# One core's hybrid decoder layer: an opening over two HGRN2 units, and recurrences of two HGRN2 units that step together

## The chip, the core and the metric

The kernel runs on one core of a Trainium2 chip. Of the core's engines, PE (TensorE) multiplies matrices into PSUM, DVE (VectorE) and ACT (ScalarE) do elementwise work, POOL (GpSimd) fills tiles, and SP (SyncE) issues most of the DMA transfers. The metric is the time of one execution on the device, in microseconds (us).

## The reference

One decoder layer over a sequence of 2048 tokens with width 1024, in float32, for a batch of one:

```
c_act = silu(c);  mod = c_act @ w_ada + b_ada        # 1024 -> 6 x 1024: sh1, sc1, g1, sh2, sc2, g2
h = rms_norm(x) * (1 + sc1) + sh1
proj = h @ w_in     # retention q k v g | HGRN2 q f v g | GLA q k v g, low-rank gate
x = x + g1 * (concat(retention, HGRN2, GLA) * head_gain) @ w_out
h = rms_norm(x) * (1 + sc2) + sh2
x = x + g2 * conv_gated_mlp(h)
out = rms_norm(x) * final_gain
```

An HGRN2 head forgets with f = lb + (1 - lb) sigmoid(z), has the key (1 - lb) sigmoid(-z) and the query silu(q). Its recurrence is S_t = diag(f_t) S_(t-1) + k_t v_t and o_t = q_t S_t. The output of each head is normalized and multiplied with silu of its gate.

## The kernel before

The sequence is cut in 4 blocks of 512 tokens. In each block the input projection is done unit by unit, in the order h0, h1, g, h2, h3, r0, r1: four HGRN2 units of two heads, one GLA unit (in two halves), and two retention units. The activations h are held as 8 tiles of 128 channels x 512 tokens, each as a high and a low part (`high`, `low`, tiles `ha`), and weights likewise (tiles whose names begin with h and l), so that a product is three multiplications: high x high, high x low, low x high (`split3`). Low parts of weights are kept in DRAM in block 0 (`keep`) and loaded again in later blocks.

An HGRN2 unit (`unit_h`) multiplies f (`pshfh`) and q (`pshqh`) in the layout channels x tokens, and value and gate (`psvgh`) in the layout tokens x channels. In block 0, value and gate of the first two units go unit by unit with 256 columns (`tf_gemm`); all other pairs go together with 512 columns (`tf512`). `tok_evac` and `tok_evac4` copy them out of PSUM: the value by ACT, the gate by ACT (sigmoid) and DVE (product).

The recurrence (`gated`) is a chain of small steps: the products with a token's own key, the dots (`dth`), seven levels with strides 1, 2, ..., 64 (`lvh`, each needing DVE's products of the level before on q and k, `qbh` and `kh`; its result goes by a masked copy into `ath`), the transposed key (`kTh`), the state's updates (`uh`, `S`), the output (`oh`), its normalization (`post`, with a Newton iteration on DVE) and its transposition (`oTh`). A planner, the class `Clock`, adds up modelled TensorE times of the projections as they are written down and inserts the next step of the chain when it is due. One chain runs at a time; the next waits in a line. PE's order is the order in which this is written; DVE, ACT and SP are ordered by a scheduler with priorities, except in the opening.

The opening (`startup`) is written out by hand for PE, DVE, ACT and SP. The condition is loaded as 128 equal rows (`craw`, 512 KB) and squashed on ACT and DVE (`c_act`). `cond(m)` multiplies it with a weight tile `wada` and sums, on DVE; 16 of the 48 such products lie in the opening. The squares of x are made by ACT and added up by DVE in a chain (`san`); TensorE sums them over the channels (`ssn`), DVE makes the reciprocal root (`rsn`), TensorE spreads it (`bcn`), and ACT copies it (`bc`). Then, for the 8 channel tiles k in turn, come scale, high part, low part, and the products of unit h0 (f, q, value and gate) with that tile. Unit h1's products follow from the general code.

PSUM has 4 banks `acc`, 2 `lev` and 2 `late`. Weights have 3 buffers each for high and low parts.

Of the kernel before, what the change touches and what calls it, by code (L numbers as in the profile page):

```python
# [4 lines left out]

# [13 lines left out]
P = 128  # L19
# [32 lines left out]
LEVEL_GAP = (3.2, 4.8)  # L52
# [50 lines left out]
def trunk(ctx, tc, xT, vecs, cvec, cst, rope, msk, wada, win, walow, wgla, wout, wup, wdown, out):  # L103
# [39 lines left out]
    nc.sync.dma_start(vec[:], vecs)  # L143
# [7 lines left out]
    nc.sync.dma_start(c_all[:], cst)  # L151
# [35 lines left out]
    def ada_load(m, early):  # L187
        if early:
            raw = pa.tile([P, D], F32, tag="a4k", name=f"wada{m}")
        else:  # L190
# [85 lines left out]
    def tf_gemm(name, i):  # L276
        if name in ready:
            return ready.pop(name)
        pss = [acc_ps(f"ps{name}_{j}") for j in range(NCH // 2)]
        for half in range(2):  # L280
            hi, lo = piece(win[i + half], f"{name}_{half}", f"i{i + half}")
            for c in range(NCH):
                o = pss[c // 2][:, (c % 2) * 256:(c % 2) * 256 + 256]
                for kk in range(4):
                    k = half * 4 + kk
                    sl = slice(kk * 256, (kk + 1) * 256)
                    cs = slice(c * P, (c + 1) * P)
                    split3(o, (h[k][:, 0, cs], h[k][:, 1, cs]), (hi[:, sl], lo[:, sl]),
                           k == 0 and c % 2 == 0, k == KD - 1 and c % 2 == 1)
                    if kk % 2:  # L290
                        adv(6 * M256)
        return pss

    def tf512(name, i, step=2):

        pss = [acc_ps(f"ps{name}_{c}") for c in range(NCH)]
        for q4 in range(4):
            half, sub = q4 // 2, q4 % 2
            src = win[i + half:i + half + step + 1:step][:, :, sub * 512:(sub + 1) * 512].rearrange("a p n -> p a n")
            with tc.high_priority(offset=50):  # L300
# [7 lines left out]
                one = [f"i{i + half + step * a}l" for a in range(2)]  # L308
                if key in kept:
                    nc.sync.dma_start(flat.bitcast(F32), kept[key][:])  # L310
                elif one[0] in kept:
                    for a in range(2):
                        nc.sync.dma_start(lo[:, a, :].bitcast(F32), kept[one[a]][:, sub * 512:(sub + 1) * 512])
                else:
                    with tc.high_priority(offset=HOT):
                        V.tensor_tensor(lo[:], raw[:], hi[:], op=ALU.subtract)
                    keep(key, flat)
# [70 lines left out]
    def startup():  # L388


        x, W, pending = [], {}, []
        for k in range(KD):
            x.append(x_tile(f"x0_{k}", k))
            nc.sync.dma_start(x[k], xT[0, :, k, :])
        raws = {}

        def weight(name, i, extra=False):
            raw = pw.tile([P, 1024], F32, tag="wraw", name="r" + name, bufs=NRAW)
            nc.sync.dma_start(raw[:], win[i])
            if extra:  # L400
                t = [pa.tile([P, 1024], F32R, tag="a4k", name=n + name) for n in "hl"]
            else:
                t = [pw.tile([P, 1024], F32R, tag="w" + n, name=n[0] + name) for n in ("hi", "lo")]
            W[name] = [*t, raw, i]

        def cast(name):
            S.copy(W[name][0][:], W[name][2][:])

        def low_part(name):
            hi, lo, raw, i = W[name]  # L410
            V.tensor_tensor(lo[:], raw[:], hi[:], op=ALU.subtract)
# [4 lines left out]
        def load(*ms):  # L416
            for m in ms:
                raws[m] = ada_load(m, True)
        load(8, 0)
        weight("f", 1)  # L420
# [7 lines left out]
        ps = late_ps("ssn1_0")  # L428
        for c in range(NCH):
            T.matmul(ps[:, c:c + 1], acc[:, c * P:(c + 1) * P], ones, start=True, stop=True)  # L430
# [3 lines left out]
        cast("f")  # L434
        bc = bc1[0] = new_bc1(0)
        ps = late_ps("bcn1_0")
        for c in range(NCH):
            T.transpose(ps[:, c * P:(c + 1) * P], r[:, c:c + 1].to_broadcast([P, P]), ident)
        cond(0)
        cond(9)  # L440
        S.copy(bc[:], ps[:])
        cast("q")
        pf, pq = acc_ps("pshfh0_0"), acc_ps("pshqh0_0")
        pv = [acc_ps(f"psvgh0_0_{j}") for j in range(NCH // 2)]

        def put(kind, k, w):

            two = (0, 1) if w == 0 else (0,)
            if kind in "fq":
                sl = slice(k * P, (k + 1) * P)  # L450
                for p in two:
                    T.matmul((pf if kind == "f" else pq)[:], W[kind][w][:, sl], h[k][:, p, :],
                             start=k == 0 and w == 0 and p == 0, stop=k == KD - 1 and w == 1, skip_group_check=True)
            else:
                sl = slice((k % 4) * 256, (k % 4 + 1) * 256)
                for c in range(NCH):
                    for p in two:
                        T.matmul(pv[c // 2][:, (c % 2) * 256:(c % 2) * 256 + 256], h[k][:, p, c * P:(c + 1) * P],
                                 W[f"v{k // 4}"][w][:, sl], start=k == 0 and w == 0 and p == 0 and c % 2 == 0,
                                 stop=k == KD - 1 and w == 1 and c % 2 == 1, skip_group_check=True)  # L460

        def flush():
            for q in list(pending):
                if (q[0] if q[0] in "fq" else f"v{q[1] // 4}") in parts[q[2]]:
# [3 lines left out]
        plan = [((10,), (), (1,), "f"), ((3, 11), (), (2,), "q"), ((4,), (10,), (3,), "v0"),  # L468
                ((12, 5), (11,), (4,), None), ((13, 6), (12,), (5,), "v1"), ((14, 7), (13,), (6,), None),
                ((15,), (14,), (7,), None), ((), (15,), (), None)]  # L470
        parts = {"f", "q"}, set()
        for k, (ld, first, then, wl) in enumerate(plan):
            if k == 0:
                weight("v0", 2)
            if k == 3:
                weight("v1", 3, True)
            load(*ld)
            for m in first:
                cond(m)
            scaled(x[k], bc[:], k)  # L480
            high(x[k], k, "0_")
            if k in (1, 4):
                name = "v0" if k == 1 else "v1"
                cast(name)
                parts[0].add(name)
            for m in then:
                cond(m)
            low(x[k], k)
            if wl:
                low_part(wl)  # L490
                parts[1].add(wl)
            pending += [(kind, k, w) for w in (0, 1) for kind in "fqv"]
            flush()
        assert not pending
        ready["hfh0_0"], ready["hqh0_0"], ready["vgh0_0"] = pf, pq, pv
# [47 lines left out]

    def tok_evac(vsg, pss):
        v, sg = vsg
        for j, ps in enumerate(pss):
            p3 = ps[:].rearrange("p (c n) -> p c n", n=256)
            c2 = slice(2 * j, 2 * j + 2)
            S.copy(v[:, c2, :], p3[:, :, 0:P])
# [1075 lines left out]
```

## Time and profile before

| | |
|---|---|
| median of 3 runs | 2557.72 us (2553.83 to 2558.8) |
| profiled execution | 2554.22 us, of which the span 2552.4 us |
| granted TensorE clock, mean | 0.993 |
| busy: PE / DVE / ACT / POOL | 97% / 78% / 45% / 6% |
| chain that ended last | PE 82%, DVE 8%, DMA 5% |

The span goes from the first to the last instruction of the profiled execution. Rows of the timeline give start, duration, engine, line, operation, the tiles written and read, the shapes, and in brackets the idle time before and what ended it. Rows of groups give the busy time of all, the mean in ns of one, then the idle time of the engine before them and what ended it; "x8" is a count. Rows of waits give engine, line, what was waited for, the sum, the number and the longest. Line numbers are those of the kernel before.

### The profile page before, as it was taken

Reading aid. Unit: us, or ns where it says so; the run is one execution under the profiler, and the core shown is the slowest. Engines: PE = TensorE matmul, PEld = TensorE weight load, DVE = VectorE, ACT = ScalarE, POOL = GpSimd, SP = SyncE. Lnnn points to the kernel's source line nnn. Section 1 sums busy time; section 2 is a strip of 40 time slices with the busy share of each in tenths; the row PEclk is TensorE's granted clock in tenths of the full one; section 3 lists DMA queues with packets and bytes.
Section 4 is the critical chain, followed back from the end, with each engine's and each line's share of the span. In section 5 each row is a group of like instructions: output and inputs, shape, how many; then the busy total and the mean of one; then the engine's idle time right before and its main releaser. Section 6 shows DMA issues by size and latency. Waiting matters only on the chain.

```text
span 2552.4 us, 35707 instructions
## 1 busy us (share of the span) xinstructions
PE 2480.7 (97%) x12418; PEld 2088.8 (82%) x12418; DVE 1986.5 (78%) x3654; ACT 1138.9 (45%) x1946; POOL 164.1 (6%) x287
## 2 busy tenths in 40 slices
PE   5999999999999999999999999999999999999998
PEld 4888887888888888888788888888878888888887
DVE  8987887878588685876798888887678778778666
ACT  3333334434353343434464555555445555455442
POOL 1000000000000000000110000000001001000000
PEclk9999999999999999999999999999999999999999
DMA  8843558864689645887655445487675544547663
GB/s 311 284 156 127 167 171 315 291 221 158 201 285 306 215 166 189 305 296 243 203 169 179 152 145 165 145 271 242 215 227 175 156 145 146 148 142 255 217 193 129
DMA packets 233028, 525.05 MB, mean 206 GB/s; under 512 B 25456, under 2 KB 28560, under 8 KB 232848
## 3 DMA queue, kind: packets, MB, share of 16 engines
q1 hardware_dynamic: 229648, 512.28, 60.9%
q0 software_dynamic: 3200, 10.49, 1.2%
q8 instruction: 98, 1.61, 0.3%
q14 instruction: 82, 0.67, 0.1%
HBM read 397.37 MB, written 125.30 MB: 205 GB/s over the span
## 4 chain that ended last, share of the span: by engine, by line
PE 82%; DVE 8%; DMA 5%; issue 1%; ACT 1%; SPq 0%; DVEq 0%; POOL 0%; ACTq 0%; POOLq 0%
PE X L254 6%; PE X L256 6%; PE X L255 6%; PE lvh L637 3%; PE Z L255 3%; PE Z L256 3%; PE Z L254 3%; PE dX L254 3%; PE dX L255 3%; PE dX L256 3%; PE psqkvgr L254 2%; PE psqkvgr L256 2%; PE psqkvgr L255 2%; PE dY L254 2%; PE dY L256 2%; PE dY L255 2%
## 5 line engine op out<-in xcount | busy, mean ns | idle before, releaser
L254 PE MATMUL X<-B,A 128*128 128x512 f32 x572 | 223.4, 391 | 1.4 <-ACT u L1332 1.4
L256 PE MATMUL X<-B,A 128*128 128x512 f32 x572 | 222.8, 390 | 0.0
L255 PE MATMUL X<-B,A 128*128 128x512 f32 x572 | 222.8, 390 | 0.0
L1038 DVE TENSOR_TENSOR dA<-rd,dA 128x512 fp32r<-128x512 f32 x154 | 106.1, 690 | 87.2 <-ACT dA L1037 86.8
L1037 ACT CAST dA<-rd 128x512 fp32r<-128x512 f32 x154 | 95.8, 622 | 140.6 <-PE dY L256 45.7
L1038 DVE TENSOR_TENSOR A<-s,A 128x512 fp32r<-128x512 f32 x176 | 120.6, 686 | 37.8 <-ACT A L1037 37.5
L1037 ACT CAST A<-s 128x512 fp32r<-128x512 f32 x176 | 108.8, 618 | 66.1 <-PE Z L256 43.5
L254 PE MATMUL dX<-dB,dA 128*128 128x512 f32 x352 | 136.9, 389 | 0.0
L255 PE MATMUL dX<-dB,dA 128*128 128x512 f32 x352 | 136.9, 389 | 0.0
L256 PE MATMUL dX<-dB,dA 128*128 128x512 f32 x352 | 136.9, 389 | 0.0
L254 PEld LDWEIGHTS X<-B,A 128*128 128x128 f32 x572 | 107.7, 188 | 24.4 <-ACT u L1332 2.2
L256 PEld LDWEIGHTS X<-B,A 128*128 128x128 f32 x572 | 107.5, 188 | 22.4
L255 PEld LDWEIGHTS X<-B,A 128*128 128x128 f32 x572 | 107.6, 188 | 22.2
L637 PEld LDWEIGHTS lvh<-qbh,kh 128*128 128x128 f32 x896 | 116.3, 191 | 10.7 <-issue 3.5
L255 PE MATMUL Z<-B,A 128*128 128x512 f32 x308 | 120.1, 390 | 2.7 <-DVE B L1038 2.7
L637 PE MATMUL lvh<-qbh,kh 128*128 128x128 f32 x896 | 120.5, 277 | 2.1 <-DVE kh L647 2.0
L254 PE MATMUL Z<-B,A 128*128 128x512 f32 x308 | 119.9, 389 | 0.0
L256 PE MATMUL Z<-B,A 128*128 128x512 f32 x308 | 119.8, 389 | 0.0
L1038 DVE TENSOR_TENSOR dB<-rb,dB 128x512 fp32r<-128x512 f32 x154 | 105.6, 687 | 9.8 <-ACT dB L1037 9.8
L254 PE MATMUL psqkvgr<-hqkvgr,ha 128*128 128x512 f32 x256 | 106.6, 416 | 4.6 <-DVE orsg L160 4.6
L1038 DVE TENSOR_TENSOR A<-r,A 128x512 fp32r<-128x512 f32 x130 | 89.4, 688 | 26.7 <-ACT A L1037 26.7
L1037 ACT CAST A<-r 128x512 fp32r<-128x512 f32 x130 | 81.0, 623 | 61.6 <-PE Z L256 59.4
(461 smaller groups left out, 7021.0 us busy)
## 6 DMA issues: line engine op xcount, KB each, us to landing
gs<-yv SPq DMA_DIRECT2D x154, 256.0 KB, 3.0
rb<-gs SPq DMA_DIRECT2D x154, 256.0 KB, 4.1
r<-wup SPq DMA_DIRECT2D x140, 256.0 KB, 3.5
s<-sumsu SPq DMA_DIRECT2D x136, 256.0 KB, 3.2
wada<-wada SPq DMA_DIRECT2D x48, 512.0 KB, 5.6
rd<-sumsd SPq DMA_DIRECT2D x88, 256.0 KB, 3.9
rd<-wdown SPq DMA_DIRECT2D x66, 256.0 KB, 3.9
x<-xT SPq DMA_DIRECT2D x64, 256.0 KB, 5.7
```

Of the source, the lines that this page charges most:

```text
L254: T.matmul(ps, lhs[0], rhs[0], start=first, stop=False, skip_group_check=more)
L255: T.matmul(ps, lhs[0], rhs[1], start=False, stop=False, skip_group_check=more)
L256: T.matmul(ps, lhs[1], rhs[0], start=False, stop=last, skip_group_check=more)
L637: T.matmul(ps[:, c * P:(c + 1) * P].rearrange("p (h n s) -> p h n s", h=2, s=s), kq[:, c * P:(c + 1) * P], rhs, start=True, stop=True)
L1037: S.copy(hi, src)
L1038: V.tensor_tensor(lo, src, hi, op=ALU.subtract)
```

## The change

**The prelude.** The condition comes as a tile of 128 x 8 (`ccol`, one DMA of single elements), is squashed on that tile, and spread by 8 transposes on TensorE and two copies by ACT. The vectors (`vec`) and constants (`c_all`) are loaded from POOL's queue instead of SP's. x comes by 4 DMAs of two tiles each. DVE adds only two squares each, and TensorE sums the four results into one bank (16 small products instead of 4). The first two scalings read the spread root from PSUM and don't wait for its copy.

**The opening.** It does f and q of h0 and h1, and their value and gate together with 512 columns, in an order written out: `scale(k)` (scale and high part), `rest(k)` (low part, then every product whose parts are there), `get(name)` and `lows(name)` (high and low part of a weight). `tf_gemm` and `tok_evac` are gone.

PE's order at the opening's first chunks before (`hf`, `lf`, `hq`, `lq`: parts of h0's weights for f and q; `hv`, `lv`: its value and gate):

```order
L452 MATMUL pshfh_0_429<-ha_0_440,hf 128x512 x2
L452 MATMUL pshqh_0_430<-ha_0_440,hq 128x512 x2
L452 MATMUL pshfh_0_429<-ha_0_440,lf 128x512
L458 MATMUL psvgh_0_0_431<-hv_435,ha_0_440 128x256 x4
L458 MATMUL psvgh_0_1_432<-hv_435,ha_0_440 128x256 x4
L452 MATMUL pshqh_0_430<-ha_0_440,lq 128x512
L452 MATMUL pshfh_0_429<-ha_1_455,hf 128x512 x2
L452 MATMUL pshqh_0_430<-ha_1_455,hq 128x512 x2
L458 MATMUL psvgh_0_0_431<-hv_435,ha_1_455 128x256 x4
L458 MATMUL psvgh_0_1_432<-hv_435,ha_1_455 128x256 x4
L452 MATMUL pshfh_0_429<-ha_1_455,lf 128x512
L452 MATMUL pshqh_0_430<-ha_1_455,lq 128x512
```

PE's order at the same place now (`pshfh_0` and `hf_372` are h0's, `pshfh_1` and `hf_457` h1's):

```order
L456 MATMUL pshfh_0_447<-ha_0_452,hf_372 128x512 x2
L456 MATMUL pshqh_0_448<-ha_0_452,hq_378 128x512 x2
L456 MATMUL pshfh_0_447<-ha_0_452,lf_373 128x512
L456 MATMUL pshqh_0_448<-ha_0_452,lq_379 128x512
L456 MATMUL pshfh_0_447<-ha_1_473,hf_372 128x512 x2
L456 MATMUL pshqh_0_448<-ha_1_473,hq_378 128x512 x2
L456 MATMUL pshfh_0_447<-ha_1_473,lf_373 128x512
L456 MATMUL pshqh_0_448<-ha_1_473,lq_379 128x512
L456 MATMUL pshfh_1_449<-ha_0_452,hf_457 128x512 x2
L456 MATMUL pshfh_1_449<-ha_1_473,hf_457 128x512 x2
L456 MATMUL pshfh_0_447<-ha_2_495,hf_372 128x512 x2
L456 MATMUL pshqh_0_448<-ha_2_495,hq_378 128x512 x2
```

Value and gate come in only after the fourth chunk; in their place stands f of h1, and behind it q of h1.

**The recurrences.** `gated` takes a list of units. h0 and h1 give one chain, h2 and h3 another, each starting after the odd unit's f and q: at every level the products of both units stand one behind the other. `LEVEL_GAP` is 4.8 for all, instead of 3.2 for a single unit.

ACT's order behind the opening now, from the copy of GLA's low-rank gate `alg` on (`hvgg`: high parts of GLA's value and gate weights; `kg`: GLA's key; `vh_1`, `sgh_1`: value and gate of h1):

```order
L832 COPY alg_877<-alg_860 32x512
L291 CAST hvgg_0_1046<-rvgg_0_1044 128x1024
L291 CAST hvgg_1_1097<-rvgg_1_1095 128x1024
L834 ACTIVATE kg_857<-psakg_889 128x512
L607 COPY vh_1_831<-psvgh_1_0_566 128x128
L608 ACTIVATE sgh_1_832<-psvgh_1_0_566 128x128
L607 COPY vh_1_831<-psvgh_1_1_567 128x128
L608 ACTIVATE sgh_1_832<-psvgh_1_1_567 128x128
L607 COPY vh_1_831<-psvgh_1_2_568 128x128
L608 ACTIVATE sgh_1_832<-psvgh_1_2_568 128x128
L607 COPY vh_1_831<-psvgh_1_3_569 128x128
L608 ACTIVATE sgh_1_832<-psvgh_1_3_569 128x128
```

The copies of h1 out of PSUM stand behind the second `hvgg` cast and `kg`; before, they stood ahead of both.

PE's order at the same place now, from the end of GLA's key (`psakg`) on:

```order
L258 MATMUL psakg_889<-ha_6_667,lakg_880 128x512
L256 MATMUL psakg_889<-ha_7_711,hakg_879 128x512
L257 MATMUL psakg_889<-ha_7_711,hakg_879 128x512
L258 MATMUL psakg_889<-ha_7_711,lakg_880 128x512
L675 MATMUL dth_0_916<-c_all,qkh_0_789 128x2 x4
L675 MATMUL dth_1_925<-c_all,qkh_1_817 128x2 x4
L687 MATMUL lvh_0_1_932<-qbh_0_791,kh_0_777 128x128 x4
L687 MATMUL lvh_1_1_937<-qbh_1_819,kh_1_805 128x128 x4
L256 MATMUL psaqg_960<-ha_0_452,haqg_949 128x512
L257 MATMUL psaqg_960<-ha_0_452,haqg_949 128x512
```

The dots and level 1 of both units stand directly behind `psakg`; before, unit h0's stood among the products of h1.

PE's order at the start of block 1 before (`or`: output of retention; `oTr`: its transposition; `pshfh_1`: f of h1):

```order
L256 MATMUL pshfh_1_3177<-ha_4_2690,lhfh_1_3172 128x512
L579 MATMUL oTr_0_3226<-c_all,or_0_3062 128x128 x4
L626 MATMUL dth_0_3236<-c_all,qkh_0_3152 128x2 x4
L637 MATMUL lvh_0_1_3243<-qbh_0_3154,kh_0_2991 128x128 x4
L254 MATMUL pshfh_1_3177<-ha_5_2696,hhfh_1_3171 128x512
L255 MATMUL pshfh_1_3177<-ha_5_2696,hhfh_1_3171 128x512
L256 MATMUL pshfh_1_3177<-ha_5_2696,lhfh_1_3172 128x512
L254 MATMUL pshfh_1_3177<-ha_6_2702,hhfh_1_3171 128x512
L255 MATMUL pshfh_1_3177<-ha_6_2702,hhfh_1_3171 128x512
L256 MATMUL pshfh_1_3177<-ha_6_2702,lhfh_1_3172 128x512
L254 MATMUL pshfh_1_3177<-ha_7_2708,hhfh_1_3171 128x512
```

PE's order at the same place now (`pshqh_1`: q of h1):

```order
L258 MATMUL pshqh_1_3131<-ha_6_2580,lhqh_1_3126 128x512
L628 MATMUL oTr_0_3203<-c_all,or_0_3050 128x128 x4
L256 MATMUL pshqh_1_3131<-ha_7_2586,hhqh_1_3125 128x512
L257 MATMUL pshqh_1_3131<-ha_7_2586,hhqh_1_3125 128x512
L258 MATMUL pshqh_1_3131<-ha_7_2586,lhqh_1_3126 128x512
L675 MATMUL dth_0_3235<-c_all,qkh_0_3000 128x2 x4
L675 MATMUL dth_1_3244<-c_all,qkh_1_3217 128x2 x4
L687 MATMUL lvh_0_1_3251<-qbh_0_3002,kh_0_2808 128x128 x4
L687 MATMUL lvh_1_1_3256<-qbh_1_3219,kh_1_3016 128x128 x4
L628 MATMUL oTr_1_3267<-c_all,or_1_3179 128x128 x4
L687 MATMUL lvh_0_2_3275<-qbh_0_3002,kh_0_2808 128x128 x4
L687 MATMUL lvh_1_2_3280<-qbh_1_3219,kh_1_3016 128x128 x4
```

The dots and the first two levels of h0 and h1 follow each other behind h1's last q products, where one unit's first level had products of h1 behind it.

The diff, cut to its core:

```diff
-LEVEL_GAP = (3.2, 4.8)
+LEVEL_GAP = 4.8
...
-    nc.sync.dma_start(vec[:], vecs)
+    ccol = pc.tile([P, KD], F32, tag="ccol", name="ccol")
+    with nc.allow_non_contiguous_dma("one row of the condition as columns"):
+        nc.sync.dma_start(ccol[:], cvec.rearrange("o (k p) -> p (o k)", p=P))
+    nc.gpsimd.dma_start(vec[:], vecs)
...
-    nc.sync.dma_start(c_all[:], cst)
+    nc.gpsimd.dma_start(c_all[:], cst)
...
-    craw = pa.tile([P, D], F32, tag="a4k", name="craw")
-    nc.sync.dma_start(craw[:], cvec.to_broadcast([P, D]))
-    S.activation(c_act[:], craw[:], AF.Sigmoid)
-    V.tensor_tensor(c_act[:], c_act[:], craw[:], op=ALU.mult)
...
+        sg = small("csg")
+        S.activation(sg[:], ccol[:], AF.Sigmoid)
+        V.tensor_tensor(ccol[:], ccol[:], sg[:], op=ALU.mult)
+        for j in range(2):
+            ps = lev_ps(f"cb{j}")
+            for n in range(4):
+                T.transpose(ps[:, n * P:(n + 1) * P], ccol[:, 4 * j + n:4 * j + n + 1].to_broadcast([P, P]), ident)
+            S.copy(c_act[:, j * 512:(j + 1) * 512], ps[:])
+        load(8)
+        load(0)
+        weight("f0")
         load(9)
-        weight("q", 0)
-        load(1, 2)
-        acc = new_acc("n1_0")
-        for k in range(KD):
-            sumsq(acc, x[k], k, "n1_0_")
+        weight("q0")
+        load(1, 1)
+        ps = late_ps("ssn1_0")
+        for j in range(4):
+            sq = [tmp(f"sq0_{j}_{n}") for n in range(2)]
+            for n in range(2):
+                S.activation(sq[n][:], x[2 * j + n], AF.Square)
+            V.tensor_tensor(sq[0][:], sq[0][:], sq[1][:], op=ALU.add)
+            for c in range(NCH):
+                T.matmul(ps[:, c:c + 1], sq[0][:, c * P:(c + 1) * P], ones, start=j == 0 and c == 0,
+                         stop=j == 3 and c == NCH - 1, skip_group_check=True)
...
+        def scale(k):
+            scaled(x[k], bps[:] if k < 2 else bc[:], k)
             high(x[k], k, "0_")
+
+        def rest(k):
             low(x[k], k)
+            pending.extend((kind, k, w) for w in (0, 1) for kind in ("f0", "q0", "f1", "q1", "v"))
             flush()
+
+        def lows(name):
+            low_part(name)
+            flush()
+
+        def get(name):
+            cast(name)
+            flush()
+
+        scale(0)
+        lows("f0")
+        weight("f1")
+        get("q0")
+        rest(0)
+        cond(9)
+        load(11)
+        cond(1)
+        load(3, 1)
+        scale(1)
+        lows("q0")
+        weight("q1")
+        rest(1)
+        cond(10)
+        load(12)
+        cond(2)
+        load(4)
+        scale(2)
+        get("f1")
...
+        get("v3")
+        lows("v3")
+        rest(7)
...
         for li, s in enumerate(LEVELS):
+            for one in parts:
+                one.pss = []
+                for q, rows, v, sg in one.subs:
+                    ps = lev_ps(f"lv{one.name}_{s}")
+                    for c in range(NCH):
+                        rhs = q[:, :, c * P:(c + 1) * P].rearrange("p h (n t s) -> p h n t s", t=2, s=s)[:, :, :, 1, :]
+                        T.matmul(ps[:, c * P:(c + 1) * P].rearrange("p (h n s) -> p h n s", h=2, s=s),
+                                 one.kq[:, c * P:(c + 1) * P], rhs, start=True, stop=True)
+                    one.pss.append(ps)
...
             with tc.high_priority(offset=CHAIN):
+                for one in parts:
+                    ev = one.tree[li]
+                    for q, rows, v, sg in one.subs:
+                        qv = q[:].rearrange("p h (n t s) -> p h n t s", t=2, s=s)[:, :, :, 1, :]
+                        V.tensor_tensor(qv, qv, ev[:, :, 0:1].unsqueeze(1).to_broadcast([P, 2, nn, s]), op=ALU.mult)
+                    kv = one.kq[:].rearrange("p (n t s) -> p n t s", t=2, s=s)[:, :, 0, :]
+                    V.tensor_tensor(kv, kv, ev[:, :, 1:2].to_broadcast([P, nn, s]), op=ALU.mult)
...
+            adv(4 * n * MF)
+            yield LEVEL_GAP
...
-        clock.chain(gated(nm, b, u, pos, kq, decay, subs, qk, selh), 9.0 if b == u == 0 else 6.0)
-        if b == 0 and u < 2:
-            tok_evac(subs[0][2:], tf_gemm("vg" + nm, 4 * u + 2))
-            tokens.add(nm)
-            return
+        half.append(SimpleNamespace(name=nm, ui=u, pos=pos, kq=kq, tree=decay[0], cur=decay[1], subs=subs, qk=qk,
+                                    sel=selh))
+        if u % 2:
+            clock.chain(gated(nm, b, [half.pop(0), half.pop(0)]), 9.0 if b == 0 and u == 1 else 6.0)
```

More of the change, by code (lines that the diff above doesn't have):

```diff
@@ new lines, in startup @@
+        weight("v1")
+        rest(3)
+        cond(12)
+        load(14)
+        cond(4)
+        load(6)
+        scale(4)
+        get("v0")
+        lows("v0")
+        weight("v2")
+        rest(4)
+        cond(13)
+        load(15)
+        cond(5)
+        load(7, 1)
+        scale(5)
+        get("v1")
+        cond(14)
+        rest(5)
+        lows("v1")
+        weight("v3")
+        cond(6)
+        scale(6)
+        get("v2")
+        cond(15)
+        rest(6)
+        lows("v2")
@@ L649, in gated @@
+                for ps, at in ((ps, at) for one in parts for ps, at in zip(one.pss, one.attns)):
                     dst = at[:].rearrange("p (a n t s) -> p a n t s", a=8, t=2, s=s)[:, :, :, 1, :]
```

285 lines of the change are left out of this document (122 added, 163 removed).

## The prediction

> **What bounds the kernel now.** I read the page first (the engines and the 40 slices).
>
> ```profile
> span 2552.4 us, 35707 instructions
> PE 2480.7 (97%) x12418; PEld 2088.8 (82%) x12418; DVE 1986.5 (78%) x3654; ACT 1138.9 (45%) x1946; POOL 164.1 (6%) x287
> PE   5999999999999999999999999999999999999998
> ```
>
> TensorE bounds it: it is busy for 97%, and of 40 slices only the first, 64 us long, stands at 5. So a change can win in two ways: less TensorE work, or less of the time in which TensorE waits or runs slowly. The table by stretches says where that time is (start and end, length, then busy time and count of PE, PEld, DVE, ACT, POOL, the granted clock, the DMA share and GB/s); after it I went to the groups by line, the timeline and TensorE's waits.
>
> ```profile
> 0.00:22.28 22.28, 2.98 (x12) 2.50 (x13) 14.77 (x34) 12.22 (x17) 8.29 (x19) 1.00 0.86 310
> 22.28:29.38 7.10, 2.87 (x5) 1.41 (x5) 6.06 (x10) 1.91 (x3) 0.00 (x0) 1.00 0.52 189
> 29.38:58.41 29.03, 25.12 (x140) 21.24 (x140) 26.32 (x38) 8.43 (x12) 1.92 (x2) 1.00 0.89 335
> 58.41:86.05 27.64, 27.23 (x184) 25.16 (x185) 26.82 (x52) 8.17 (x15) 0.00 (x0) 1.00 0.87 305
> 58.41:1240.00 1181.59, 1162.59 (x6523) 998.86 (x6524) 922.18 (x2146) 459.42 (x891) 59.80 (x101) 0.99 0.67 226
> 344.00:352.00 8.00, 6.43 (x39) 5.42 (x38) 8.00 (x20) 2.01 (x3) 0.00 (x0) 1.00 0.36 131
> ```
>
> No weight is multiplied before 22.28 us; five multiplications fit into the next 7.1 us. From 29.38 to 58.41 VectorE is busy for 26.32 of 29.03 us: there TensorE is fed at VectorE's pace. From 58.41 to 1240 us, the other attention work, TensorE idles for only 1181.59 - 1162.59 = 19.0 us: that is all that better stepping can win there, but for the slow clock behind a stall.
>
> **Part 1: up to the first multiplication.** The rows of VectorE around it:
>
> ```profile
> L358 DVE TENSOR_TENSOR san<-san,sqn 128x512 f32<-128x512 f32 x7 | 4.8, 692 | 0.8
> L357 ACT ACTIVATE sqn<-x 128x512 f32<-128x512 f32 x7 | 4.4, 630 | 0.8 <-DVE san L358 0.7
> 19.52 1.28 DVE L199 CUSTOM_DVE_ANT_0 wada<-wada,c_act,vec 128x1024 f32<-128x1024 f32 x1
> 20.72 0.75 DVE L364 SCALAR_TENSOR_TENSOR x<-x,mod,bc 128x512 f32<-128x512 f32 x1
> ```
>
> Three of seven additions go (2.1 us of VectorE), but ScalarE now does a small sigmoid, two copies out of the transposes and eight squares, 8 x 0.63 = 5.0 us, one behind the other; the squares end at about the time at which the additions ended. I take no gain there. Behind the reciprocal root one conditioning product (1.28, the row at 19.52) no longer stands ahead of the first scaling. I take 1.1 us: first multiplication at 21.2 instead of 22.28. Bounds: 2.1 us won if the additions set the pace, 1.5 lost if the constants, which now come over POOL's queue, arrive late at the transposes.
>
> **Part 2: the opening's products.** Spacings of TensorE, full and slow, are read from the timeline:
>
> ```profile
> 59.20 0.39 PE L254 MATMUL pshfh<-ha,hhfh 128*128 128x512 f32 x1
> 63.96 0.39 PE L254 MATMUL pshqh<-ha,hhqh 128*128 128x512 f32 x1
> 68.04 0.95 PE L626 MATMUL dth<-c_all,qkh 128*128 128x2 f32 x8
> 85.69 0.28 PE L254 MATMUL psvgh<-hvgh,ha 128*128 128x256 f32 x1
> 85.81 0.28 PE L255 MATMUL psvgh<-lvgh,ha 128*128 128x256 f32 x1
> 86.05 0.39 PE L773 MATMUL alg<-ha,alow 128*32 128x512 f32 x1
> 169.61 0.68 PE L579 MATMUL oTh<-c_all,oh 128*128 128x128 f32 x4 [3.02 <-DVE oh L573]
> ...
> 170.52 0.63 PE L255 MATMUL pshqh<-ha,hhqh 128*128 128x512 f32 x1
> 170.95 0.63 PE L256 MATMUL pshqh<-ha,lhqh 128*128 128x512 f32 x1
> ...
> 173.74 0.40 PE L254 MATMUL pshqh<-ha,hhqh 128*128 128x512 f32 x1
> 173.97 0.39 PE L255 MATMUL pshqh<-ha,hhqh 128*128 128x512 f32 x1
> ```
>
> 21 multiplications of 512 columns lie between 59.20 and 63.96: 0.227 us each. One of 256 columns takes 0.12 (85.69, 85.81). Before, both HGRN2 units' products are done when `alg` starts at 86.05; in between stand pieces of unit 0's recurrence (dots 0.95, 32 level multiplications and their wait), about 4.6 us that move to later. So the point to compare with is 81.4. After, the same products are 2 x 48 of f and q and 96 of value and gate, all of 512 columns: 192 x 0.227 = 43.6 us (before, with 256 columns, 2 x (48 x 0.227 + 96 x 0.12) = 44.8).
>
> Slow time: behind the wait of 3.02 us at 169.61 the spacing is 0.43 (170.52 to 170.95) until about 173.5; then 0.23 again. So a stall of some 3 us costs about 1.7 us more behind it. VectorE's list decides how many there are after:
>
> ```profile
> L199 DVE CUSTOM_DVE_ANT_0 wada<-wada,c_act,vec 128x1024 f32<-128x1024 f32 x14 | 17.9, 1279 | 1.2 <-DMA wada<-wada 1.2
> L364 DVE SCALAR_TENSOR_TENSOR x<-x,mod,bc 128x512 f32<-128x512 f32 x8 | 6.0, 750 | 0.2
> L371 DVE SCALAR_TENSOR_TENSOR ha<-x,mod,ha 128x512 fp32r<-128x512 f32 x8 | 6.0, 747 | 0.0
> L411 DVE TENSOR_TENSOR lf<-rf,hf 128x1024 fp32r<-128x1024 f32 x1 | 1.2, 1219 | 0.0
> ```
>
> After: 14 conditioning products, 8 scalings, 8 low halves of h and 8 of weights, 17.9 + 6.0 + 6.0 + 8 x 1.22 = 39.7 us of busy time, from 20.1 on: with overlap and some 4 us of waits for casts it ends near 62. The chunks k = 0 to 2 hold 9 x 3 + 3 multiplications, less than VectorE needs for them: I work out two gaps of some 2.5 us (before q0's low half, and at f1's high half, whose cast stands behind that of h[2] on ScalarE), slow clock until about 36, and 1 us at the first value weight. 21.2 + 43.6 + 6.0 of gaps + half of the 9.8 us that run slow, 4.9, is 75.7: 76 against 81.4, **-5.4**. Bounds: with full clock throughout TensorE waits for VectorE's end at 62 plus the last 24 products (5.5), 68: -13. If the slow clock holds until 50, +7 on top: +1.6.
>
> By the Trainium skill (TensorE: Matmul & The Clock Gate, Part 1), the array falls to half rate after an idle window of about 3.4 us and needs about 3.4 us of work for the full rate. The trace agrees in the second (170.0 to 173.5). By the first, gaps of 2.5 us alone need not cool it, and the sum of this part would be nearer -9; I keep -5.4, since the array starts cold.
>
> **Part 3: dots of the first pair.** Behind the opening TensorE does 16 `alg`, 24 `psakg`, then the dots `dth0_0`. These need a PSUM bank that held value/gate of the pair; the copies out of unit 1's half stand on ScalarE behind the cast `hvgg0_1`, which overwrites the weight buffer that `psakg` reads last, and VectorE's `lvgg0_1` stands in the same way before unit 0's last gate products.
>
> ```profile
> L305 ACT CAST hvgg<-rvgg 128x1024 fp32r<-128x1024 f32 x3 | 3.2, 1051 | 2.9 <-PE psaqg L255 2.9
> L316 DVE TENSOR_TENSOR lvgg<-rvgg,hvgg 128x1024 fp32r<-128x1024 f32 x4 | 4.9, 1223 | 0.0
> L558 ACT COPY vh<-psvgh 128x128 f32<-128x128 f32 x8 | 2.1, 266 | 1.0 <-DVE sgh L560 0.7 <-PE psvgh L256 0.3
> L559 ACT ACTIVATE sgh<-psvgh 128x128 f32<-128x128 f32 x8 | 2.3, 288 | 0.0
> ```
>
> So the dots come at psakg's end + 1.05 + 1.15 + three pairs of 0.55 + VectorE's products of 0.4 to 0.7, about 4.5 us, in which TensorE has nothing else in its order; with the slow clock behind it (1.9), **+6.4**. Bounds: 0 if the copies get done before that cast, +8.
>
> **Part 4: start of block 1.** Before, only unit 0's level 1 stands there, with 24 products of unit 1 behind it; TensorE waits 1.57 at the second level pair. After, both units' dots and levels 1 and 2 follow unit 1's last q products with nothing but `oTr` between.
>
> ```profile
> 349.93 1.13 PE L637 MATMUL lvh<-qbh,kh 128*128 128x128 f32 x8 [1.57 <-DVE kh L647]
> L659 DVE COPY_PREDICATED ath<-m_all,lvh 128x512 f32<-128x512 uint32 x80 | 75.8, 947 | 0.0
> L645 DVE TENSOR_TENSOR qbh<-qbh,eh 128x512 f32<-128x512 f32 x96 | 66.0, 688 | 27.2 <-PE lvh L637 26.7
> L647 DVE TENSOR_TENSOR kh<-kh,eh 128x256 f32<-128x256 f32 x96 | 40.2, 418 | 0.0
> ```
>
> A level of a pair costs VectorE 2 x (0.69 + 0.42 + 0.95) = 4.1 us. From `or0_1` on VectorE owes retention's normalization (about 4.7), unit 1's gating (sqh, qkh, two qbh halves: 2.7), a weight's low half (1.2) and the first level, some 12 us, against some 4.5 us of TensorE work in the order: a wait of 6 to 8, of which before had 1.6, plus slow clock: **+5.5**. Bounds +1 (VectorE had done the gating earlier) and +9.
>
> **Part 5: the rest.** Two units in step leave VectorE fewer holes; TensorE's spacing of levels goes from two chains of 7 levels to one. Before's stalls there, of which the largest follow, may go or come again elsewhere:
>
> ```profile
> PE oTh L579 <- DVE oh L573: 3.0, 1, 3.0
> PE psvgh L254 <- DVE sqh L732: 2.6, 1, 2.6
> PE psqkvgr L254 <- DVE orsg L160: 4.6, 2, 2.7
> ```
>
> I take half of these 10.2 us, **-5**; bounds -15 (all 19.0 us but 4) and +4 (blocks 2 and 3 get new ones like part 4's). The loads on POOL's queue, the one DMA instead of two for kept low halves, and 16 instead of 4 one-column products cost nothing: DMA stands at shares under 0.9, and the one-column products lie under ScalarE's squares. From the channel mixer on nothing changes.
>
> **Sum.** -5.4 + 6.4 + 5.5 - 5 = +1.5 on the profiled execution's 2554.22, that is 2555.7; the median of the runs is 3.5 above that profile, so 2559 against it. I say 2558.
>
> **Rivals.**
> - *Faster: the opening keeps up and the stalls of parts 3 and 4 are half as long.* For it: VectorE would end at 62 and TensorE could be done at 68. Against: the order has nothing to fill the two waits. -9 + 3 + 3 - 6 = -9: 2549.
> - *Slower: VectorE at the start of block 1.* If the 12 us of VectorE's list there come in full after `or0_1`, and the same repeats once more where a pair starts (parts 3 and 4 at +8 and +9 with the slow clock, the rest at -3, the opening at -5), the sum is +9: 2567. It decides from a wait of 7 us on at that place. For it: VectorE is busy for all of 8.00 us there before (the row from 344). Against: levels may be taken ahead of other work.
> - *The change does little of what it says*: the order behind the first pair stays the same as before, the waits too; -5 alone, 2552 to 2558.
>
> By a rule on another page of the Trainium skill (DMA: Bandwidth & Descriptors, the at-a-glance table), a load issued by GpSimd has its first byte after about 1 us against 0.6 for SyncE, and pieces under 512 bytes fall behind line rate; the 1024 single elements of the condition and the constants would come later by that, and part 1 would be -0.5. No run here shows it.
>
> **How the numbers follow.** The forecast (terms cancel, 2551 to 2565) gets 0.42: 0.28 of it within 0.2%, 0.04 faster, 0.10 slower. The faster rival gets 0.31, the slower 0.24, the last 0.03 (0.02 of it same, 0.01 faster). That makes faster 0.36, same 0.30, slower 0.34; 0.2%, 5 us, is about what the runs tell from no change, since the three shown span 5.0 us. The range goes from 2545, below the faster rival, to 2568, just above the slower one.
>
> **What would show it.** Right: first multiplication near 21, `alg` near 76, spacing 0.43 until about 36; a wait of about 4.5 us of `dth` for `sgh`'s product behind `psakg`; waits of 6 to 8 us in sum between `or0_1` and block 1's second level. The forecast is wrong if `alg` starts under 70 or over 80, if TensorE's idle time from there to the channel mixer is under 12 us or over 35, or if VectorE's queue, not ScalarE's, is what the dots wait for.

## The result and the profile after

The changed kernel took 2652.43 us (median of 4 runs, 2650.65 to 2654.35), the kernel before 2555.99 beside it. The ratio is 1.0377, with a 95% interval of 1.0359 to 1.0395: 96 us slower, where 2558 was forecast with 2568 as the upper end. From the page of the kernel after:

```profile
span 2652.3 us, 35615 instructions
PE 2529.5 (95%) x12354; PEld 2128.4 (80%) x12354; DVE 1999.9 (75%) x3655; ACT 1139.3 (43%) x1956; POOL 164.6 (6%) x289
PE   6988989999899999999899999999999999999998
PEclk9998979999899999999999999999999999999999
```

TensorE issues 64 instructions fewer and is busy 49 us longer; the granted clock now has an 8 and a 7 in the first six slices, where before it was 9 throughout. To find the place, both executions are cut at the starts of `alg`, GLA's low-rank gate of each block, and at the first product of the up-projection (X). After:

```profile
25.02:80.02 55.00, 49.02 (x192) 38.49 (x193) 42.09 (x62) 15.26 (x20) 7.88 (x12) 1.00 0.92 321
80.02:450.62 370.60, 338.10 (x1787) 290.21 (x1786) 293.29 (x641) 127.37 (x254) 13.88 (x24) 0.92 0.49 167
450.62:776.08 325.46, 306.00 (x1668) 262.46 (x1667) 231.56 (x543) 121.00 (x233) 15.67 (x26) 0.97 0.63 212
776.08:1097.08 321.00, 308.11 (x1671) 264.14 (x1670) 231.51 (x545) 121.13 (x234) 15.67 (x26) 0.97 0.66 224
1097.08:1330.21 233.13, 221.20 (x1227) 189.71 (x1226) 173.83 (x409) 84.51 (x172) 12.07 (x23) 0.97 0.70 240
```

The same cuts of before:

```profile
86.05:402.16 316.11, 306.77 (x1684) 260.71 (x1682) 257.95 (x575) 117.63 (x225) 15.80 (x26) 0.98 0.54 182
402.16:706.32 304.16, 299.94 (x1670) 258.07 (x1671) 228.53 (x544) 122.64 (x238) 15.80 (x26) 0.99 0.69 232
706.32:1007.00 300.68, 297.99 (x1671) 256.16 (x1670) 228.55 (x545) 120.74 (x234) 15.80 (x26) 1.00 0.71 239
1007.00:1233.00 226.00, 223.66 (x1287) 192.96 (x1286) 175.73 (x416) 87.35 (x178) 12.27 (x22) 0.99 0.74 254
```

The opening is 6.0 us shorter (86.05 to 80.02). Block 0 from there on is 54.5 longer (316.1 to 370.6), the next two cuts 21.3 and 20.3, the last 7.1; with 2.7 in the channel mixer that is the 99.9 us between the spans. Part of this is work that lies elsewhere now: in the first cut TensorE has some 100 more of the small products for dots and levels (h0's of block 0, which lay ahead of it before, and h1's of block 1, which lay behind it), in the last 60 fewer. By the prediction's 4.6 us for 40 of them that is an estimated 12 us more and 7 us less. In the first cut TensorE idles for 32.5 us (before 9.3) and its granted clock is 0.92 (before 0.98). From the list of TensorE's waits over the whole execution after (9.1, 5.0, 4.5 and 3.7 lie in the first cut, 7.7 lies in block 1):

```profile
PE oTh L628 <- DVE S L930: 11.2, 4, 4.0
PE psqkvgr L256 <- DVE sgr L609: 9.1, 1, 9.1
...
PE or L642 <- DVE oTh L632: 7.7, 1, 7.7
...
PE psvgh L256 <- DVE sqh L788: 5.0, 1, 5.0
PE dth L675 <- DVE sgh L609: 4.5, 1, 4.5
...
PE dth L675 <- DVE nw L163: 3.7, 1, 3.7
...
```

These end at VectorE, as most of the list does. One was forecast to the tenth (4.5, the first dots), and most others were not forecast at all. From `alg` to the channel mixer TensorE idles for 76.8 us (before 18.6), and the four cuts are 103 us longer in sum; most of the rest is the slower clock behind the waits.

### The profile page after: what moved, and what is told of

The parts are those of the page before. It is cut to its first block, busy times and chain, and to the rows that moved or that the text cites. A ratio compares the mean times of both kernels' runs of the same rounds, so it can differ in the third digit from the quotient of the medians.

```text
span 2652.3 us, 35615 instructions
## 1 busy us (share of the span) xinstructions
PE 2529.5 (95%) x12354; PEld 2128.4 (80%) x12354; DVE 1999.9 (75%) x3655; ACT 1139.3 (43%) x1956; POOL 164.6 (6%) x289
```

## The experiments

Where the kernels' profiled executions stand at the cuts (starts of `alg` in blocks 0 to 3, then X), and the median of their runs:

| kernel | alg 0 | alg 1 | alg 2 | alg 3 | X | us |
|---|---|---|---|---|---|---|
| before | 86 | 402 | 706 | 1007 | 1233 | 2556 |
| after | 80 | 451 | 776 | 1097 | 1330 | 2652 |
| e1 pairs, old opening | 85 | 412 | 732 | 1055 | 1286 | 2609 |
| e2 new opening, one pair | 80 | 442 | 748 | 1053 | 1279 | 2605 |
| e5 old opening, late start | 84 | 440 | 746 | 1052 | 1274 | 2597 |
| e6 after, short Newton | 80 | 443 | 763 | 1081 | 1306 | 2628 |
| e10 new opening, caught up | 80 | 408 | 712 | 1015 | 1240 | 2566 |
| e12 e1, copies first | 85 | 416 | 735 | 1053 | 1286 | 2606 |

**Which half of the change.** Pairs alone (e1):

```diff
 # kernel before, opening unchanged
-        clock.chain(gated(nm, b, u, pos, kq, decay, subs, qk, selh), 9.0 if b == u == 0 else 6.0)
+        half.append(SimpleNamespace(...))
+        if u % 2:
+            clock.chain(gated(nm, b, [half.pop(0), half.pop(0)]), 9.0 if b == 0 and u == 1 else 6.0)
```

> The opening of before, with the recurrences of h0 and h1, and of h2 and h3, stepping together as in the changed kernel. Theory P (the pairing costs the time: two units' state updates, normalizations and transpositions come at once, at the end of a block where VectorE has no holes): 2635 to 2660 us, nearly all of the loss of 96. Rival O (the new opening costs it, by what it delays behind itself): 2550 to 2565.

Measured: 2608.69, ratio 1.0203 (1.0186 to 1.0219).

The new opening, with one pair (e2):

```diff
 # kernel after
-        if u % 2:
+        if not (b == 0 and u < 2):
+            clock.chain(gated(nm, b, [half.pop(0)]), 6.0)
+        elif u % 2:
             clock.chain(gated(nm, b, [half.pop(0), half.pop(0)]), 9.0 if b == 0 and u == 1 else 6.0)
...
-            yield LEVEL_GAP
+            yield LEVEL_GAP if n > 1 else 3.2
```

> The new opening, h0 and h1 as a pair in block 0 alone, every other HGRN2 unit in a chain of its own with the old gap of 3.2. Theory P: the blocks 1 to 3 and the end of block 0 come back to before, 2560 to 2585 (what is left is the stall behind the opening and block 0's pair). Rival O: 2640 to 2655.

Measured: 2605.18, ratio 1.0192 (1.0164 to 1.0220). Both theories were half right: each half costs about 50 us, and 53 + 50 is about the 96 of the whole. In the table e2 stands 40 us behind the kernel before at block 1's `alg` (442 against 402) and loses 6 more up to X (306 and 305 us a block, before 304 and 301). Its profiled execution, at 2612 the longest of four, loses another 12 behind X, where retention's last transposition now comes after X's first product. e1 loses 10 up to block 1's `alg` and then 15, 22 and 5 in the three cuts behind it; of the 10 most are again dots and levels that stand ahead of this `alg` now (some 70 more products in the first cut, 60 fewer in the last).

The condition in e2, `b == 0 and u < 2`, made `u < 2` (e3): pairs of h0 and h1 in all blocks.

> The changed kernel with h0 and h1 as a pair in all four blocks, h2 and h3 in chains of their own. If the end of a block is the place (pair of h2 and h3 running into retention): 2585 to 2610. If the start of a block is (both units' dots and levels behind h1's q): 2630 to 2645. If the two cost alike: about 2615.

Measured: 2599.47, ratio 1.0165 (1.0146 to 1.0184). It is no slower than e2, so the pair at a block's start is not what costs. The pair of h2 and h3 is: with it, in the kernel after, the time is 53 us longer. The old opening with pairs of h0 and h1 in blocks 1 to 3 alone (`b and u < 2`, e8) fits that:

> The opening and block 0 of before; in blocks 1 to 3 h0 and h1 as a pair, h2 and h3 in chains of their own. By the difference of the two kernels with the new opening (2599 with these pairs, 2605 without): 2546 to 2556. If a pair costs at the start of a block what it costs at the end: 2580 to 2600.

Measured: 2559.38 against 2553.32, ratio 1.0022 (1.0013 to 1.0031), 3 us above the expected range: a loss of 6 us, and no gain. In the traces block 1's `alg` comes 8 us later with this pair (450 in e3 against 442 in e2, 411 in e8 against 402 before), since h1's levels stand ahead of it then; by X most of that is made up (1275 against 1279, 1237 against 1233).

**The first dots.** In the changed kernel (e4):

```diff
-                tok_evac4(waiting.pop(one), pss, 256 * i)
+                with tc.high_priority(offset=HOT if b == 0 and u == 1 else 0):
+                    tok_evac4(waiting.pop(one), pss, 256 * i)
```

> The changed kernel, with the copies of h0's and h1's value and gate out of PSUM put ahead of the hvgg cast in block 0. If the wait of 4.5 us of the dots is what part 3 of the prediction says: it goes, with the slow clock behind it, and the time falls by 5 to 7 us, 2645 to 2648. If another wait takes its place: 2652 within 3.

Measured: 2642.58, 10 us less than the kernel after (9 when each is compared with the kernel before beside it), and no wait of the first dots is left. That is some 3 us more than the 6.4 of the wait and its slow clock, a first sign that an early loss grows.

**The line of recurrences.** One number in the kernel before (e5):

```diff
-9.0 if b == u == 0 else 6.0
+22.0 if b == u == 0 else 6.0
```

> The kernel before, with one number changed: the first recurrence (h0 in block 0) starts 13 us later by the planner's clock. Theory L (the recurrences stand in one line that is about as long as a block's projections, so what its start loses comes back as waits at the end of block 0): 2563 to 2571, lost before block 1's low-rank gate starts. Rival (the line has slack): 2553 to 2558.

Measured: 2596.96, ratio 1.0163 (1.0145 to 1.0181): 43.6 us for a start that came 14.5 us later on TensorE. Theory L was right in kind and a factor of three short in size. The chain's position shows how it grows: retention's first step `qTr` in block 0 stands at the end of that line. In before and in e5, the first rows of the timeline for it:

```profile
304.33 0.61 PE L849 MATMUL qTr<-c_all,ra0r 128*128 128x128 f32 x4
```

```profile
82.54 0.95 PE L626 MATMUL dth<-c_all,qkh 128*128 128x2 f32 x8
345.16 0.61 PE L849 MATMUL qTr<-c_all,ra0r 128*128 128x128 f32 x4
```

Started at 82.5 instead of 68.0, it arrives 40.8 late. (The profiled execution of e5, 2604.73 us, is the longest of its four.) The delay grows from unit to unit, as the starts of each one's dots show:

| | h0 | h1 | g | h2 | h3 | `qTr` |
|---|---|---|---|---|---|---|
| before | 68.0 | 109.1 | 149.1 | 225.2 | 264.6 | 304.3 |
| e5 | 82.5 | 123.1 | 169.4 | 250.5 | 298.4 | 345.2 |
| later by | 14.5 | 14.0 | 20.3 | 25.2 | 33.8 | 40.8 |

TensorE's largest waits of e5 between the first two cuts; the second and the third stand in the kernel after too (9.1 and 1.9 there):

```profile
PE ssn L337 <- DVE eh L610: 6.9, 1, 6.9
PE psqkvgr L254 <- DVE sgr L560: 5.8, 1, 5.8
PE pshfh L254 <- DVE sgg L560: 4.2, 1, 4.2
PE oTr L579 <- DVE or L573: 3.9, 1, 3.9
```

Two of them are projections (`psqkvgr`, `pshfh`) that wait until value and gate leave PSUM. ScalarE's rows before the wait of 9.1 in the kernel after and before that of 5.8 in e5 say what those copies wait for in turn:

```profile
254.49 0.79 ACT L608 ACTIVATE sgr<-psqkvgr 128x128 f32<-128x128 f32 x4 [6.82 <-DVE og L622]
257.53 0.79 ACT L559 ACTIVATE sgr<-psqkvgr 128x128 f32<-128x128 f32 x4 [5.10 <-DVE og L573]
```

`og` at L622 (L573 in e5) is the last reader of GLA's gate. The gates have 4 buffers; h2, h3 and GLA's two halves hold them until their recurrences are done. So a late line stops the projections, and these hold up its next steps on TensorE. No run has more of these buffers, so their share in the 41 us stays open.

The start alone does not decide; what counts is where the line stands later on. In e1 it starts 11.6 us later than before (79.7); but as two units step in one chain there, GLA's dots come at 151.4 (before 149.1) and `qTr` at 302.4, not late at all. In the kernel after GLA's dots come at 174.1 and `qTr` at 344.6, much as in e5.

Then the line in the new opening was made to catch up (e9): e2 and e4 together, with smaller gaps between the first pair's levels.

```diff
-            yield LEVEL_GAP if n > 1 else 3.2
+            yield (2.4 if b == 0 and parts[0].ui == 0 else LEVEL_GAP) if n > 1 else 3.2
```

> The new opening with one pair (h0 and h1 in block 0), chains of one unit elsewhere, as in the kernel that took 2605; in addition the copies of value and gate ahead of the hvgg cast, and the planner's gap between the levels of that first pair 2.4 instead of 4.8, so that the line of recurrences is some 20 us earlier from the end of that pair on. Theory L (what the opening costs is the late start of the line): 2555 to 2575, with the waits at the end of block 0 mostly gone. Rival (the opening's order costs by itself, or VectorE can't step faster): 2588 to 2600.

Measured: 2574.71, ratio 1.0074 (1.0058 to 1.0089), 30 less than e2. With 9.0 changed to 3.0 for the pair's start (e10):

> The same, with the first pair due 6 us earlier by the planner (3.0 instead of 9.0 after h1's products). Theory L: another 3 to 10 us if the line was still late, nothing if it had caught up; 2550 to 2570. Rival: a new wait of the dots for the copies out of PSUM takes it back, within 2 of the run before.

Measured: 2565.80, ratio 1.0045 (1.0030 to 1.0059), another 9 less. From its timeline and its waits in block 0:

```profile
306.46 0.61 PE L908 MATMUL qTr<-c_all,ra0r 128*128 128x128 f32 x4
```

```profile
PE dth L675 <- DVE qkh L790: 7.6, 2, 5.2
PE psqkvgr L256 <- DVE orsg L164: 3.0, 1, 3.0
PE ssn L319 <- DVE san L340: 2.2, 1, 2.2
```

`qTr` is back within 2.1 us of before, and of the 50 us 10 are left. So some 40 of the opening's 50 us were the line's. The 7.6 us for which the pair's dots wait belong to the new order itself. No run starts the line of the kernel before earlier, so whether that one would gain from it too is open.

**The pair at a block's end.** From retention's first `qTr` in block 2 backwards and forwards, as a table by stretches: 20 us ahead of it, then up to the transposition of retention's first output, `oTr`. Before:

```profile
885.00:905.10 20.10, 20.10 (x117) 17.42 (x116) 15.17 (x37) 9.92 (x26) 0.13 (x1) 1.00 0.64 206
905.10:933.60 28.50, 28.50 (x172) 25.22 (x172) 27.44 (x71) 13.37 (x20) 5.78 (x10) 1.00 0.46 154
```

e1, pairs with the old opening:

```profile
901.00:921.00 20.00, 20.00 (x125) 17.71 (x124) 9.21 (x33) 5.35 (x13) 1.19 (x3) 1.00 0.42 134
921.00:962.00 41.00, 33.42 (x176) 28.74 (x174) 35.50 (x89) 16.90 (x31) 3.90 (x8) 0.89 0.39 132
```

VectorE's updates of the pair's states in the first stretch of e1:

```profile
L695 DVE SCALAR_TENSOR_TENSOR S<-S,eh,uh 64x64 f32<-64x64 f32 x16 | 4.5, 281 | 9.6 <-PE uh L685 9.2
```

Ahead of `qTr` VectorE has 9.2 us of work instead of 15.2: the pair's state updates wait for TensorE's, one unit after the other, and the first output is there only 5 us before the stretch ends. Behind it VectorE has 35.5 instead of 27.4. By its lines, some 5 of these 8 us are retention's rotations (`ra`, `rb`), which before were done ahead of `qTr`, some 2 the next block's scalings, and 1 the heads' second output. Before, TensorE is busy for all of the 28.5 us of the stretch; in e1 it lasts 41.0, and TensorE idles for 7.6 of them. Less work for VectorE there, first in the kernel after (e6) and then in before (e7):

```diff
-        for _ in range(3):
+        for _ in range(rounds):        # 1 in the heads' normalization, 3 elsewhere
```

> The changed kernel with one round instead of three in the Newton iteration of the heads' normalization (which leaves out two of three rounds, 6 small VectorE instructions of about 0.2 us in each of 8 normalizations of a block). Theory V (where the two units' normalizations come at the end of a block, VectorE's queue sets the end): 15 to 35 us faster, 2617 to 2637, most of it at the ends of the blocks. Rival (TensorE's order or PSUM banks set it): 0 to 6 faster.

> The same edit on the kernel before, as the control. Theory V: the same instructions are covered there, 0 to 6 us faster, 2549 to 2556. If they are as dear there as in the changed kernel, the edit says nothing about pairing.

Measured: 2627.50, 25 less than after; the control 2554.37, ratio 1.0006 (0.9991 to 1.0022). The same instructions are worth 25 us in the kernel after and nothing in the kernel before. But by the table some 8 of the 25 came in block 0, and blocks 1 and 2 stay 320 and 318 long against 304 and 301: shorter iterations mend a quarter or less of what the pairs cost there, and 8 more at the end of block 3.

The rival to a mere excess of work was the order in the queues of VectorE and ScalarE: in block 1 of the kernel after, retention's output `or` waits 7.7 us for `oTh`, whose copies out of both late banks stand among the next block's scalings and behind most of them. e1 has the same wait; e1 with one edit (e12):

```diff
-        S.activation(oT[:, 0, :], ps[:], AF.Copy, scale=hg)
-        V.scalar_tensor_tensor(oT[:, 1, :], ps[:], hg, oT[:, 0, :], op0=ALU.mult, op1=ALU.subtract)
+        with tc.high_priority(offset=CHAIN):
+            S.activation(oT[:, 0, :], ps[:], AF.Copy, scale=hg)
+            V.scalar_tensor_tensor(oT[:, 1, :], ps[:], hg, oT[:, 0, :], op0=ALU.mult, op1=ALU.subtract)
```

> The kernel with the old opening and pairs everywhere (2609), with one edit: the two instructions that take a transposed output out of PSUM (oTh, oTr) come ahead of the next block's scaling in ScalarE's and VectorE's queues. Theory B (at a block's end both late banks hold outputs of the pair, whose copies stand on VectorE behind the next block's scalings, so retention's output on TensorE waits): the wait of 7.7 us in block 1 and its slow clock go, in the other blocks the shorter ones, 2575 to 2592. Rival V (VectorE has too much to do there in sum, whatever its order): 2604 to 2612.

> The same edit on the kernel before, as the control. Theory B: with one unit's output at a time one late bank stays free, so the copy's place is worth little: 2548 to 2558. If the edit helps every kernel alike: 2535 or less.

Measured: 2605.79, ratio 1.0211 (1.0196 to 1.0227), as without the edit; the control (e13) 2555.72, ratio 1.0011 (1.0000 to 1.0022). The waits of `or` are gone, and others stand in their place. TensorE's waits at the end of block 2 in e1, then in e12:

```profile
PE or L594 <- DVE orsr L161: 3.1, 1, 3.1
PE oTh L580 <- DVE S L886: 2.7, 1, 2.7
```

```profile
PE oTr L580 <- DVE orsr L156: 4.3, 1, 4.3
PE oTh L580 <- DVE S L887: 2.7, 1, 2.7
```

In block 1, the place that the theory named, the 7.7 us are gone, `oTr` waits 3.8 and `oTh` 3.4 instead of 2.7, and the block takes 318.8 us instead of 319.2. So theory B fell: the wait went and the time stayed, since the copies come first and the normalization later. That fits the sum of VectorE's work in that stretch as the cause, but doesn't show it: VectorE is idle for 5.5 of the 41.0 us in e1, and for 1.1 of the 28.5 before. How much of the 50 us comes from the steps one behind the other (state update, output, square, normalization) no run separated.

**The sums of squares.** In the changed kernel (e11), the four tiles added up on VectorE and four products instead of sixteen:

```diff
+            if j:
+                V.tensor_tensor(sq[0][:], sq[0][:], last[:], op=ALU.add)
+            last = sq[0]
-            for c in range(NCH):
-                T.matmul(ps[:, c:c + 1], sq[0][:, c * P:(c + 1) * P], ones, ...)
+        for c in range(NCH):
+            T.matmul(ps[:, c:c + 1], last[:, c * P:(c + 1) * P], ones, start=True, stop=True)
```

> The changed kernel with the four tiles of squares added up by VectorE again and four one-column products (eight instructions) instead of sixteen. If those products cost about 0.22 us for each of their 32 instructions on the path, as the profile after shows: VectorE's mean square statistics (msn) start 1.0 to 2.2 us earlier, and the first product of a weight at 22.8 to 24.0 instead of 25.0 us. If the squares by ScalarE set the pace: no change.

Measured, in a single execution (2645.72 us): statistics at 18.88 instead of 19.50 us, the first weight's product at 24.39 instead of 25.02: 0.6, less than expected, since the three additions take 0.7 each behind the squares. All mends together (e14):

> The new opening with what the runs point to: one pair in block 0, with its copies first, its gap 2.4 and its start 3.0 (2566), the four one-column sums, and the transposed outputs copied first. By the sum of the single gains (0.6 and at most 4): 2560 to 2566. Faster than before (under 2551) only if the stall of the dots at 86 to 98 us shrinks as well, which nothing here does.

Measured: 2564.74, ratio 1.0041 (1.0029 to 1.0053), in the expected range, but not to be told from e10 (1.0045): the last two mends gave nothing that these runs can show. No version beat the kernel before.

## Why the prediction was wrong

*Part 1* forecast the first product at 21.2; it came at 25.0, outside the part's own bounds. The rows around it before:

```profile
2.89 0.16 DVE L167 TENSOR_TENSOR lbe<-vec 128x4 f32<-128x4 f32 x1 [2.89 <-DMA vec<-vecs]
8.84 5.47 DVE L358 TENSOR_TENSOR san<-san,sqn 128x512 f32<-128x512 f32 x7
```

After:

```profile
5.88 0.16 DVE L171 TENSOR_TENSOR lbe<-vec 128x4 f32<-128x4 f32 x1 [5.88 <-DMA vec<-vecs]
10.54 4.46 ACT L429 ACTIVATE sq<-x 128x512 f32<-128x512 f32 x8
12.47 6.99 PE L432 MATMUL ssn<-c_all,sq 128*128 128x1 f32 x32 [2.45 <-DVE sq L430]
15.04 0.69 DVE L430 TENSOR_TENSOR sq<-sq,sq 128x512 f32<-128x512 f32 x1 [0.55 <-ACT sq L429]
19.50 0.16 DVE L436 TENSOR_SCALAR msn<-ssn 128x4 f32<-128x4 f32 x1 [2.56 <-PE ssn L432]
23.46 0.75 DVE L346 SCALAR_TENSOR_TENSOR x<-x,mod,bcn 128x512 f32<-128x512 f32 x1 [0.62 <-ACT bc L443]
25.02 0.79 PE L456 MATMUL pshfh<-ha,hf 128*128 128x512 f32 x1 [2.21 <-ACT ha L350]
```

Two steps failed. "The squares end at about the time at which the additions ended" was 1.4 us off: the last addition ends at 15.7 instead of 14.3, since ScalarE squares from 10.5 on (before from 7.5). The copies of the condition stand ahead of the squares there, and ahead of those ScalarE's step on the vectors, which over POOL's queue are there at 5.9 instead of 2.9. The constants took 5.7 us from issue to landing on that queue, on SP's 2.2; but x's loads now begin ahead of both, so the queue's share is open. And "16 instead of 4 one-column products cost nothing" was 1.8 us off: they are 32 instructions and take 6.99 us, so that VectorE waits 2.56 for them, and from the last addition to the statistics it takes 3.8 us instead of 1.9. With four products e11 won back only 0.6, as three additions come onto the same path. The other 0.6 is missing behind the root, where 0.5 was gained instead of 1.1: the scaling that was to read PSUM directly still waited for ScalarE's copy of the same bank (0.62).

*Part 2* held but for that start: `alg` at 80.0 against 76, of which 3.8 are part 1's. The two gaps and the slow stretch came as worked out:

```profile
30.26 0.79 PE L456 MATMUL pshqh<-ha,lq 128*128 128x512 f32 x1 [2.13 <-DVE lq L407]
35.69 2.93 PE L456 MATMUL pshfh<-ha,hf 128*128 128x512 f32 x6 [2.07 <-ACT hf L402]
39.19 0.62 PE L456 MATMUL pshfh<-ha,hf 128*128 128x512 f32 x2
47.25 3.92 PE L464 MATMUL psvgh<-hv,ha 128*128 128x512 f32 x16 [1.53 <-ACT hv L402]
```

Gaps of 2.13, 2.07 and 1.53 were forecast as 2.5, 2.5 and 1, and the six products at 35.69 still ran at about 0.45 each, so the array was not at full rate before 39 us (forecast 36). The column of the granted clock, 1.00 from 25.02 to 80.02, does not show this stretch; the spacing of the products does. The Trainium skill (TensorE: Matmul & The Clock Gate, Part 1) asks for some 3.4 us of sustained work before the full rate. The trace agrees: the burst from 30.26 to 33.62, 3.4 us long, ended with products at 0.43, and in the next one, from 35.69 on, they are 0.23 apart from 39.19 on, 3.5 us after its start.

*Part 3* named the wait and its length, 4.5, and e4 shows that its reason was right. It priced it with the slow clock behind it at 6.4, and not what the later line costs; e4 gave 9 to 10.

*Part 4* saw the right place: 3.7 us of the dots and 5.5 in all stand there after, where 6 to 8 were forecast. But e3 and e8 show that the pair at a block's start costs little. That block 1's `alg` comes 48 us late is the line's, but for some 8 us of h1's levels, which only lie ahead of it now.

*Part 5* had the wrong sign. It let half of before's stalls go (-5); the three cuts behind block 0 lost 48.7, with less to do in the last. The pair of h2 and h3, which e3 puts the loss on, it met only with a bound of "+4", for stalls like part 4's at a block's start, and not with the end of a block. Its own sign of being wrong, more than 35 us of idle time from `alg` to the channel mixer, came with 76.8.

So two steps cost about 50 us each. One is this of part 5. The other is in part 2: "about 4.6 us that move to later", which was right as TensorE's work, but put the later start of the chain at nothing. What moved was the start of a line of steps that lasts as long as the projections beside it: the first dots went from 68.0 to 93.8. The rows of before told it, had they been read as a line: from the first dots at 68.0 to `qTr` at 304.3 one step follows another. The slower rival had the direction and VectorE as the cause, at the wrong end of the block, and at a tenth of the size. So its direction was luck.

## What to carry to other kernels

Where a chain of small steps runs beside the main work and lasts as long as it, read it as a second critical path: note when its first step starts and when its last ends, and price a later start by an experiment on that one number, since it came back threefold in e5. Steps that are bunched save nothing if the engine behind them has its holes at another time: compare the busy time of that engine in the stretch before and in the stretch behind. And count a small product by its instructions, not by its columns.

## What the runs showed of the hardware

A float32 product with one moving column took 6.99 us / 32 = 0.22 us an instruction at the opening, about as much as one with 512 columns at full rate (0.227 in the prediction's rows). About half of that was the slow clock: at full rate, in the midst of other products, eight of them take 0.81 us in the kernel before, 0.1 each.

```profile
1269.97 0.95 PE L337 MATMUL ssn<-c_all,san 128*128 128x1 f32 x8
1270.78 0.48 PE L254 MATMUL X<-hB,A 128*128 128x512 f32 x1
```

What a wait of TensorE costs behind it is not one fixed price. In the kernel after, products of 512 columns came 0.43 apart behind the wait of 2.53 us at 363.31, and 0.23 apart behind that of 2.65 us at 986.24.
